# One layer of a hybrid diffusion trunk on one core: tile order of the output projection, gate on its products, stream slots, spread gathers, norm of x on GpSimd

## The chip, the core and the metric

The kernel runs on one core of a Trainium2 chip. The core has TensorE (PE, matmuls), VectorE (DVE), ScalarE (ACT), GpSimd (POOL) and SyncE (SP, which here only issues transfers), and 16 DMA engines that fill on-chip memory (SBUF) from HBM. Matmul results land in PSUM. The metric is device time in microseconds (us) of one execution; the median of several runs is compared.

## The reference, cut to what matters

One layer (DEPTH = 1) on 512 latent tokens of width 1024, with 256 context tokens, in float32.

```python
h  = modulate(rms_norm(x, norm1_g), sh1, sc1)          # shifts, scales, gates from c @ w_mod
p  = h @ w_in                                          # q, k, v, hyena, fourier, three gates
m  = sigmoid(ga)*ya + sigmoid(gh)*yh + sigmoid(gf)*yf  # three branches @ w_branch
x  = x + g1 * (m @ w_out)                              # the output projection
h2 = modulate(rms_norm(x, norm2_g), sh2, sc2)
aff = softmax(h2 @ w_router)                           # 512 x 16
top_w, top_i = top_k(aff.T, 64)                        # each of 16 experts chooses 64 tokens
y  = (silu(h2[top_i] @ w_gate) * (h2[top_i] @ w_up)) @ w_down * top_w
x  = x + g2 * scatter_add(y)
return rms_norm(x, final_g)
```

w_gate, w_up and w_down hold 16 experts of three 1024 x 2048 matrices: 24 MB (of 2^20 bytes) per expert, 384 MB in all, each read once.

## The kernel before, in words

**Stages.** First comes an opening (lines 327 to 526) whose order on SP, ACT, DVE and PE is that of the program (`tc.manual_schedule`; POOL is not in it): the filters of the long convolution, the products of c with the first third of w_mod (`mod1`, eight blocks of 1 MB), the sums of squares of x (`square`), the inverse root (`rsqrt`, Newton steps without a table) and the scaling of x (`xscale`, even tiles on DVE, odd ones on ACT). `mrow` copies the product row out of PSUM once `mod1(7)` is done; the shifts and scales A1, B1 and then `hT` follow from it. From line 609 on a planner (the tile framework) orders each engine's instructions by its own estimate. Then come projections, long convolutions, attention and the merge (`merge`, lines 1178 to 1204).

**Output projection.** The merged rows lie as T3a (row tiles 0 and 1) and T3b (row tiles 2 and 3), each in a high and a low part; so does w_out, in four column blocks of 256: `WO[0]` in the slot T1_0, `WO[1]` in T1_1, `WO[2]` in wsp, `WO[3]` in mpart. `wo_load(q)` (line 1160) loads 1 MB of w_out, multiplies it by the gate g1 on POOL (line 1167), and splits it into high (ACT, line 234) and low (DVE, line 235). `wout(c, t)` (line 1230) does one 128 x 256 product in 24 matmuls (8 k's of three), adds it to x on DVE (line 1238) and squares it on ACT. The program first runs column blocks 0 and 1 for all four row tiles, then 2 and 3 for all. In between lie the transposes `x1T`, router products `logits`, `norm2`, `affinity`, `affT`, and `best(t)` (eight rounds of top-8 and replace on DVE; row tile 1 needs the result of row tile 0, and 2 that of 1). After the last `best` come threshold, slot numbers and the first one-hot gather.

**The weight stream.** 386 blocks, nearly all of 1 MB, numbered in the order of use: 8 of w_gate, 8 of w_up, 8 of w_down per expert (0 to 7, 8 to 15, 16 to 23 for expert 0). `loads()` (line 1098) says which slot each goes to, `prefetch` issues them on SP in that order. A load waits on SP until the slot's former content has been read, and all later loads wait behind it. Two-block slots (T2b, T2a, T1_0, T1_1, wsp, T3a, T3b) and the ring (three single blocks) come round; acc, mpart and xtra serve once. The slots hold 22 blocks at first. After that a cycle has 16 blocks, with two ring loads in it. A pair that starts at an even block is one 2 MB transfer, else it is two of 1 MB (lines 1126 to 1131). The memory of mpart becomes the pool `moe` (line 1406), in which the hidden rows of expert 0 lie.

**Experts.** `up(e)` multiplies the gathered rows with 16 blocks (line 1401), `down(e)` with 8 (line 1437). `gather(pr)` picks the rows of two experts by 64 one-hot matmuls, in eight steps (line 1372); `gather(0)` runs inside `up(0)`, every other one is run as a whole between the two experts of a pair (line 1466). After each pair the results are scattered (line 1481) and added.

Of the kernel before, what the change touches and what calls it, by code (L numbers as in the profile page):

```python
# [19 lines left out]
D = 1024  # L20
# [172 lines left out]
def _body(tc, nc, es, a, out, dbg, stop):  # L193
# [94 lines left out]
    def rsqrt(pool_, out_, ms, shape, pre, E=None, tag=""):  # L288

        E = E or V  # L290

        t, y, z = (pool_.tile(shape, F32, name="rq" + tag + n) for n in "tyz")
        E.tensor_scalar(t, ms, pre, EPS, op0=OP.mult, op1=OP.add)
        E.tensor_scalar(y.bitcast(I32), t.bitcast(I32), -0.5, float(0x5F3759DF), op0=OP.mult, op1=OP.add)

        def yyt():
            if shape[1] == 1:
                E.tensor_scalar(z, y, y, t, op0=OP.mult, op1=OP.mult)
            else:
                E.tensor_mul(z, y, y)  # L300
                E.tensor_mul(z, z, t)

        for c in (3.0, 12.0):
            yyt()
            if shape[1] == 1:
                E.tensor_scalar(y, z, c, y, op0=OP.subtract, op1=OP.mult)
            else:
                E.scalar_tensor_tensor(y, z, c, y, op0=OP.subtract, op1=OP.mult)
        yyt()
        E.tensor_scalar(z, z, -1.0 / 8192.0, 3.0 / 32.0, op0=OP.mult, op1=OP.add)  # L310
        E.tensor_mul(out_, z, y)
# [193 lines left out]
    rsqrt(ep, XR[0], MS[0], [128, 4], 1.0 / D, tag="4")  # L505
    mod1(4)
    next(sp)
    for t in range(4):
        xscale(t)
# [3 lines left out]
    drain(sp)  # L513
    mod1(7)
# [583 lines left out]
    def loads():  # L1098


        first = [("T2b", 0), ("T2a", 2), (None, 4), (None, 5), (None, 20), ("acc", 6), ("T1_0", 8), ("T1_1", 10),
                 ("T3a", 16), ("mpart", 12), ("wsp", 14), ("T3b", 18), ("xtra", 21)]
        yield from first
        j = 22
        while j < len(stream):
            for tag in ("T2b", "T2a", None, None, "T1_0", "T1_1", "wsp", "T3a", "T3b"):
                yield tag, j
                j += 1 if tag is None else 2
# [51 lines left out]
    def wo_load(q):  # L1160

# [5 lines left out]
        G.tensor_mul(w_, w_, g1b[:, None, cs_].to_broadcast([128, 8, 256]))  # L1167
# [62 lines left out]
    def wout(c, t):  # L1230
# [3 lines left out]
        for k in range(8):  # L1234
            mm3(o[:, :256], *(x_[:, k, t % 2 * 128:(t % 2 + 1) * 128] for x_ in MT[t // 2]), W[0][:, k], W[1][:, k], k == 0, k == 7)
            if k == 3:
                yield
        V.tensor_add(x1[:, t, cs_], x1[:, t, cs_], o[:, :256])
# [48 lines left out]
    for t in range(4):  # L1287
        drain(wout(0, t))
        if t:
            x1T(t - 1, 0)  # L1290
        drain(wout(1, t))
        if t:
            logits(t - 1, 0)
    prefetch(2)
    for t in range(4):
        w_ = wout(2, t)
        next(w_)
        x1T(t - 1 if t else 3, 1 if t else 0)
        drain(w_)
        if t:  # L1300
            logits(t - 1, 1)
            affinity(t - 1)
        else:
            logits(3, 0)
        drain(wout(3, t))
        if t == 1:
            prefetch(1)
        norm2(t)
        if t == 3:
            x1T(3, 1)  # L1310
        if t:
            affT(t - 1)
            best(t - 1)
    logits(3, 1)
    affinity(3)
    affT(3)
    prefetch(3)
# [70 lines left out]
    def up(e):  # L1388
        gat = gather(0) if e == 0 else iter(())
        es_ = slice((e % 2) * CAP, (e % 2 + 1) * CAP)  # L1390
        acc_ = []
        for nm in ("pa", "pu"):
            o = pbig(nm) if e < NE - 1 or nm == "pa" else [pmm(nm), pmm(nm)]
            for k in range(8):
                next(gat, None)
# [61 lines left out]
    for pr in range(8):  # L1457
# [7 lines left out]
        if pr < 7:  # L1465
            drain(gather(pr + 1))
        else:
            fgb = K1n[:, :1024]
            nc.scalar.dma_start(fgb[0:1], a["rows"][:, 1024:2048])
            spread(fgb, -0.5)  # L1470
# [99 lines left out]
```

## Time and profile before

| what | us |
|---|---|
| median of 3 runs (1482.6 to 1487.5) | 1484.34 |
| the profiled execution | 1482.58 |
| its span, first to last instruction | 1480.8 |
| PE busy | 1344.8 |
| DVE busy | 501.1 |
| ACT busy | 287.6 |
| POOL busy | 131.7 |

The profile is of one execution. Busy time is a sum over stages with different limits, so the argument goes by stage: by windows of the span, by the timeline of one engine, and by the chain of work that ended last. DMA share is the mean busy share of the 16 DMA engines; GB/s counts 10^9 bytes, so 1 MB of the stream is 1.049 of its megabytes. "Idle before <- X" names what an engine waited for.

### The profile page before, as it was taken

To read this page: it belongs to the slowest core of one execution; us is meant where nothing else is said; L and a number is where in the kernel's file an instruction comes from. 1 tells how busy PE (TensorE), PEld (TensorE's weight loads), DVE (VectorE), ACT (ScalarE), POOL (GpSimd) and SP (SyncE) were. 2 spreads that over 40 slices of the span, in tenths; PEclk is the share of its full clock that TensorE was granted. 3 is DMA by queue.
4 is the path that set the end of the run, shared out by engine and by line. 5 is a ranking of instruction groups with operands and counts; after the bars stand their busy time and mean duration, and the time that the engine had idled before them with its cause. 6 is when DMAs were issued, how large, how long until landed. Compare 5 with 4: busy or idle time off the path is not lost.

```text
span 1480.8 us, 16061 instructions
## 1 busy us (share of the span) xinstructions
PE 1344.8 (91%) x6659; PEld 713.8 (48%) x6659; DVE 501.1 (34%) x980; ACT 287.6 (19%) x513; POOL 131.7 (9%) x131
## 2 busy tenths in 40 slices
PE   5899999999998979999999889988979988989896
PEld 2666678777787953433434323323423423423233
DVE  5867677666557361121121021111101201201123
ACT  5554235444333210100000000000000000000003
POOL 2043431000114010000000000000000000000002
PEclk9999999999999989999999999999999999999998
DMA  9425795110525658899999999999999999999994
GB/s 380 179 76 154 295 307 116 58 56 30 208 90 187 249 223 337 333 430 428 429 430 432 429 430 430 430 430 431 430 431 429 430 430 430 430 430 430 429 430 193
DMA packets 50658, 478.66 MB, mean 323 GB/s; under 512 B 5517, under 2 KB 10255, under 8 KB 16666
## 3 DMA queue, kind: packets, MB, share of 16 engines
q1 hardware_dynamic: 46008, 464.20, 76.0%
q0 software_dynamic: 2752, 9.05, 2.4%
q10 hardware_dynamic: 1826, 4.40, 0.8%
q8 instruction: 52, 0.85, 0.2%
q14 instruction: 20, 0.16, 0.0%
HBM read 473.02 MB, written 4.21 MB: 322 GB/s over the span
## 4 chain that ended last, share of the span: by engine, by line
PE 50%; DMA 41%; DVE 5%; ACT 2%; issue 1%; POOL 0%; ACTq 0%; DVEq 0%; SPq 0%
DMA rawT<-in_wu_dram 11%; DMA rawT<-in_wd_dram 9%; DMA rawwsp<-in_wu_dram 7%; PE py L1437 6%; PE pmm L229 6%; PE pmm L230 6%; PE pmm L231 6%; PE pu L1401 6%; PE pa L1401 5%; DMA rawT3a<-in_wu_dram 4%; DMA rawT2a<-in_wg_dram 2%; DMA rawwsp<-in_wg_dram 2%; DMA rawT2b<-in_wu_dram 2%; PE gx L1372 2%; DMA ld<-in_wmod_dram 2%; PE pmm L1056 2%
## 5 line engine op out<-in xcount | busy, mean ns | idle before, releaser
L1415 DVE TENSOR_TENSOR hid<-hid,pu 128x512 f32<-128x512 f32 x32 | 20.6, 684 | 453.9 <-PE pu L1401 441.4
L229 PE MATMUL pmm<-T,wsp 128*128 128x512 f32 x288 | 115.6, 404 | 1.3 <-DVE ht L594 1.3
L231 PE MATMUL pmm<-T,wsp 128*128 128x512 f32 x288 | 113.3, 393 | 2.2 <-DVE wsp L235 2.2
L230 PE MATMUL pmm<-T,wsp 128*128 128x512 f32 x288 | 113.4, 394 | 1.3 <-DVE T L235 1.3
L1414 ACT ACTIVATE hid<-pa 128x512 f32<-128x512 f32 x32 | 17.4, 594 | 421.0 <-PE pa L1401 406.5
L1372 PEld LDWEIGHTS gx<-vt,x 128*128 128x128 f32 x512 | 62.2, 195 | 29.3 <-issue 18.7
L1357 POOL TENSOR_SCALAR vt<-iota,slot,rs 128x64 f32<-128x64 f32 x16 | 10.3, 669 | 735.6 <-PE stp L1452 717.0
L1372 PE MATMUL gx<-vt,x 128*128 128x128 f32 x512 | 69.8, 289 | 5.2 <-DVE vt L1357 1.9
L1443 DVE TENSOR_TENSOR Y<-py,g2b 64x512 f32<-64x512 f32 x30 | 20.7, 689 | 154.1 <-PE py L1437 139.6
L235 DVE TENSOR_TENSOR wsp<-ld,wsp 128x1024 fp32r<-128x1024 f32 (+1 forms) x39 | 54.4, 1403 | 42.3 <-ACT wsp L234 42.1
L1437 PE MATMUL py<-rawT,hidT 128*64 128x512 f32 x224 | 52.3, 612 | 14.8 <-DMA rawT<-in_wd_dram 14.8
L229 PEld LDWEIGHTS pmm<-T,wsp 128*128 128x128 f32 x288 | 53.9, 188 | 21.6 <-issue 9.5
L1481 PE MATMUL sc<-Y,st 128*128 128x512 f32 (+1 forms) x128 | 57.0, 598 | 5.6 <-DVE Y L1443 5.6
L231 PEld LDWEIGHTS pmm<-T,wsp 128*128 128x128 f32 x288 | 54.2, 188 | 16.1 <-DVE wsp L235 2.6
L230 PEld LDWEIGHTS pmm<-T,wsp 128*128 128x128 f32 x288 | 54.4, 189 | 13.6 <-DVE T L235 1.9
L1423 ACT ACTIVATE hidT<-hp 128x512 f32<-128x512 f32 x16 | 9.6, 597 | 264.4 <-PE hp L1418 145.5
L234 ACT ACTIVATE wsp<-ld 128x1024 fp32r<-128x1024 f32 (+1 forms) x39 | 41.8, 1078 | 51.8 <-PE pmm L230 30.6
L1481 PEld LDWEIGHTS sc<-Y,st 128*128 128x128 f32 (+1 forms) x128 | 23.5, 189 | 39.5 <-issue 26.4
L1485 DVE TENSOR_TENSOR acc<-acc,sc 128x512 f32<-128x512 f32 x56 | 38.2, 687 | 10.9 <-PE sc L1481 10.9
L1437 PEld LDWEIGHTS py<-rawT,hidT 128*64 128x64 f32 x224 | 16.6, 140 | 50.2 <-issue 39.3
L1401 PE MATMUL pu<-rawT,xg 128*64 128x512 f32 x128 | 32.7, 654 | 6.2 <-DMA rawT<-in_wu_dram 6.2
L1401 PE MATMUL pu<-rawT,K1n 128*64 128x512 f32 x128 | 30.7, 600 | 7.9 <-DMA rawT<-in_wu_dram 7.9
(563 smaller groups left out, 2372.9 us busy)
## 6 DMA issues: line engine op xcount, KB each, us to landing
rawT<-in_wu_dram SPq DMA_DIRECT2D x16, 2048.0 KB, 33.9
rawT<-in_wg_dram SPq DMA_DIRECT2D x16, 2048.0 KB, 34.0
rawT<-in_wd_dram SPq DMA_DIRECT2D x14, 2048.0 KB, 29.2
ld<-in_wmod_dram SPq DMA_DIRECT2D x24, 1024.0 KB, 6.7
ld<-in_win_dram SPq DMA_DIRECT2D x19, 1024.0 KB, 5.7
ld<-in_wg_dram SPq DMA_DIRECT2D x18, 1024.0 KB, 34.0
rawT2a<-in_wg_dram SPq DMA_DIRECT2D x9, 2048.0 KB, 33.5
rawwsp<-in_wu_dram SPq DMA_DIRECT2D x9, 2048.0 KB, 28.7
```

Of the source, the lines that this page charges most:

```text
L229: mm(o, ah, bh, start=first, stop=False)
L230: mm(o, ah, bl, start=False, stop=False)
L231: mm(o, al, bh, start=False, stop=last)
L234: keep(A.activation(hi, src, AF.Copy))
L235: keep((eng or V).tensor_sub(lo, src, hi.bitcast(F32)))
L1056: mm(o[64 * g:64 * g + 64], vt[:, k, kv * 64:kv * 64 + 64], PT[h - 1 + g][:, k, :], start=k == 0, stop=k == 5)
L1372: mm(o[:, k % 4], x1[:, t, k * 128:(k + 1) * 128], oh[:, t], start=t == 0, stop=t == 3)
L1401: mm(ob[64 * hf:64 * hf + 64], xg[:, k, es_], w_[:, (2 * b + hf) * 512:(2 * b + hf + 1) * 512], start=k == 0, stop=k == 7)
L1437: mm(o[64 * dh:64 * dh + 64, :], hcol(hT_, fb), w_[:, i * 1024 + dh * 512:i * 1024 + (dh + 1) * 512], start=fb == 0, stop=fb == 15)
L1443: V.tensor_mul(Y2[es2, dh * 512:(dh + 1) * 512], o[64 * dh:64 * dh + 64], M["g2b"][64 * dh:64 * dh + 64, dh * 512:(dh + 1) * 512])
L1481: mm(o, st[ks, t * 128:(t + 1) * 128], Y2[ks, ds_], start=True, stop=True)
L1485: V.tensor_add(acc[:, t, ds_], acc[:, t, ds_], o)
```

## The change

1. In the opening, `rsqrt` for x runs on POOL instead of DVE, where the fused subtract-and-multiply becomes two instructions; the four `xscale` move behind `mod1(6)` and the last filter planes.
2. `wo_load` no longer multiplies by g1. `wout` multiplies its product by g1 on DVE into a scratch tile and adds that to x: two DVE instructions instead of one.
3. The projection runs row tiles 0 and 1 through all four column blocks first. The first two products do k = 0 to 6 before either does k = 7. `x1T`, `logits`, `norm2`, `affinity`, `affT` and `best` follow each row tile as it is complete. Loads are issued as T3a, T1_0, T1_1, wsp, mpart and T3b come free, in this order.
4. The stream's slots: T3a takes blocks 6 and 7, then T1_0, T1_1, wsp, mpart, T3b take 8 to 17; acc, which serves once, takes 18 and 19. The cycle has a third ring load: 17 blocks.
5. `gather(pr + 1)` runs inside `up` of the pair's second expert, one step at every second k.

```diff
@@ rsqrt
+            elif E is G:
+                E.tensor_scalar(z, z, c, None, op0=OP.subtract)
+                E.tensor_mul(y, z, y)
@@ the opening
-    rsqrt(ep, XR[0], MS[0], [128, 4], 1.0 / D, tag="4")
+    rsqrt(ep, XR[0], MS[0], [128, 4], 1.0 / D, G, tag="4")
     mod1(4)
     next(sp)
-    for t in range(4):
-        xscale(t)
     mod1(5)
     next(sp)
     mod1(6)
     drain(sp)
+    for t in range(4):
+        xscale(t)
     mod1(7)
@@ loads
-        first = [("T2b", 0), ("T2a", 2), (None, 4), (None, 5), (None, 20), ("acc", 6), ("T1_0", 8), ("T1_1", 10),
-                 ("T3a", 16), ("mpart", 12), ("wsp", 14), ("T3b", 18), ("xtra", 21)]
+        first = [("T2b", 0), ("T2a", 2), (None, 4), (None, 5), (None, 20), ("acc", 18), ("T3a", 6), ("T1_0", 8),
+                 ("T1_1", 10), ("wsp", 12), ("mpart", 14), ("T3b", 16), ("xtra", 21)]
...
-            for tag in ("T2b", "T2a", None, None, "T1_0", "T1_1", "wsp", "T3a", "T3b"):
+            for tag in ("T2b", "T2a", None, None, "T3a", "T1_0", "T1_1", "wsp", "T3b", None):
@@ wo_load
-        G.tensor_mul(w_, w_, g1b[:, None, cs_].to_broadcast([128, 8, 256]))
@@ wout
-    def wout(c, t):
+    def wout(c, t, stop=4):
...
         for k in range(8):
+            if k == stop:
+                yield
             mm3(o[:, :256], *(x_[:, k, t % 2 * 128:(t % 2 + 1) * 128] for x_ in MT[t // 2]), W[0][:, k], W[1][:, k], k == 0, k == 7)
-            if k == 3:
-                yield
-        V.tensor_add(x1[:, t, cs_], x1[:, t, cs_], o[:, :256])
+        d_ = flat(vt)[:, (c + t) % 2 * 256:((c + t) % 2 + 1) * 256]
+        V.tensor_mul(d_, o[:, :256], g1b[:, cs_])
+        V.tensor_add(x1[:, t, cs_], x1[:, t, cs_], d_)
@@ the order (the old loops are removed)
+    w0, w1 = wout(0, 0, 7), wout(0, 1, 7)
+    for w_ in (w0, w1, w0, w1):
+        next(w_)
+    inside, behind, later = [], [], []
+    for c, t in ((1, 0), (1, 1), (2, 0), (3, 0), (2, 1), (3, 1), (0, 2), (1, 2), (2, 2), (3, 2), (0, 3), (1, 3), (2, 3), (3, 3)):
+        w_ = wout(c, t)
+        next(w_)
+        for f_, *as_ in inside:
+            f_(*as_)
+        drain(w_)
+        for f_, *as_ in behind:
+            f_(*as_)
+        inside, behind, later = [], later, []
+        if c % 2:
+            inside = [(x1T, t, c // 2)]
+            behind.append((logits, t, c // 2))
+        if c == 3:
+            norm2(t)
+            behind.append((affinity, t))
+            later = [(affT, t), (best, t)]
+        if (c, t) in ((3, 1), (0, 3), (1, 3), (2, 3)):
+            prefetch(1)
+    for f_, *as_ in inside + behind:
+        f_(*as_)
+    affT(3)
     prefetch(2)
@@ up
-        gat = gather(0) if e == 0 else iter(())
+        gat = gather(0) if e == 0 else gather(e // 2 + 1) if e % 2 and e < NE - 1 else iter(())
...
-                next(gat, None)
+                if e == 0 or k % 2:
+                    next(gat, None)
@@ between the experts of a pair
-        if pr < 7:
-            drain(gather(pr + 1))
-        else:
+        if pr == 7:
```

## Rows read from the trace of the kernel before

**Rows 1.** The page's second part: DMA busy tenths and GB/s in 40 equal slices of the span (37 us each).

```profile
DMA  9425795110525658899999999999999999999994
GB/s 380 179 76 154 295 307 116 58 56 30 208 90 187 249 223 337 333 430 428 429 430 432 429 430 430 430 430 431 430 431 429 430 430 430 430 430 430 429 430 193
```

**Rows 2.** Windows of the span: stretch, its length, busy us (and instructions) of PE, PEld, DVE, ACT, POOL, then the granted TensorE clock, DMA share, GB/s. First the start of the experts, then the stretch up to the end of the stream, then the end.

```profile
555.00:620.00 65.00, 64.17 (x332) 28.19 (x332) 10.94 (x34) 6.22 (x12) 1.28 (x2) 1.00 0.85 322
620.00:640.00 20.00, 19.15 (x90) 6.42 (x86) 1.14 (x2) 1.09 (x2) 0.00 (x0) 1.00 1.01 430
640.00:1440.00 800.00, 724.87 (x3334) 271.49 (x3334) 123.82 (x253) 40.52 (x76) 7.67 (x12) 0.99 1.01 430
...
1455.00:1460.00 5.00, 5.00 (x30) 2.87 (x30) 1.28 (x2) 3.37 (x10) 2.37 (x3) 1.00 0.31 127
```

**Rows 3.** The opening: the timeline of DVE (first and last instruction of `rsqrt`), of ACT (the two `xscale`, then `mrow`), and of POOL (the second filter sum; then first and last of the nine instructions of `norm2(1)` on POOL, much later). Columns: start us, us, engine, line, operation, out<-in, count, idle before.

```profile
35.76 0.17 DVE L293 TENSOR_SCALAR rq4t<-ms 128x4 f32<-128x4 f32 x1 [1.29 <-ACT T2b L385]
...
39.01 0.16 DVE L311 TENSOR_TENSOR xr<-rq4z,rq4y 128x4 f32<-128x4 f32 x1
...
39.21 2.19 ACT L390 ACTIVATE xa<-xa,xr 128x1024 f32<-128x1024 f32 x2 [2.99 <-DVE xr L311]
41.91 0.60 ACT L516 ACTIVATE mrow<-mod 128x512 f32<-128x512 f32 x1 [0.51 <-PE mod L366]
...
36.29 1.28 POOL L445 TENSOR_TENSOR Gt<-keep 128x512 f32<-128x512 f32 x1 [0.67 <-ACT keep L440]
...
514.68 0.20 POOL L293 TENSOR_SCALAR rqt<-ms 128x1 f32<-128x1 f32 x1 [43.08 <-DVE ms L1261]
...
517.68 0.19 POOL L311 TENSOR_TENSOR rs<-rqz,rqy 128x1 f32<-128x1 f32 x1
```

**Rows 4.** Around the last merge: the low splits of w_out blocks 0 and 1 and one add of the merge on DVE, the gate multiplications of blocks 2 and 3 on POOL, and the matmul behind PE's pause, from the engines' timelines; then a window behind it (columns as in rows 2).

```profile
457.46 2.29 DVE L235 TENSOR_TENSOR T<-ld,T 128x2048 fp32r<-128x2048 f32 x1 [1.35 <-ACT T L234]
460.40 6.00 DVE L235 TENSOR_TENSOR T<-ld,T 128x2048 fp32r<-128x2048 f32 x1 [0.64 <-ACT T L234]
...
467.03 4.27 DVE L1180 TENSOR_TENSOR mpart<-mpart,sg 128x512 f32<-128x512 f32 x1
...
472.49 0.68 DVE L1180 TENSOR_TENSOR mpart<-mpart,sg 128x512 f32<-128x512 f32 x1
...
459.49 4.76 POOL L1167 TENSOR_TENSOR ld<-ld,K1n 128x2048 f32<-128x2048 f32 x1 [5.77 <-DMA ld<-in_wout_dram]
465.04 5.72 POOL L1167 TENSOR_TENSOR ld<-ld,K1n 128x2048 f32<-128x2048 f32 x1 [0.79 <-DMA ld<-in_wout_dram]
...
471.81 0.58 PE L229 MATMUL pmm<-T,T3a 128*128 128x256 f32 x1 [6.24 <-ACT T3a L234]
...
471.80:476.40 4.60, 4.59 (x21) 4.56 (x22) 3.19 (x8) 3.45 (x5) 0.00 (x0) 0.51 0.79 337
```

**Rows 5.** The rest of the projection and the routing: a window over the last twelve of the 16 products, and one from there to the end of the last `best` (columns as in rows 2); from DVE's timeline the first and last instruction of `best(0)`, the instruction behind the last `best`, and one add of a product to x.

```profile
484.58:527.80 43.22, 43.22 (x370) 43.19 (x370) 19.22 (x87) 10.59 (x36) 4.82 (x18) 1.00 0.57 219
527.80:541.24 13.44, 8.09 (x32) 3.91 (x32) 12.26 (x65) 2.72 (x6) 0.00 (x0) 0.62 0.97 399
...
513.95 0.28 DVE L1283 MAX8 K1n<-K1n 16x8 f32<-16x128 f32 x1
...
519.60 0.26 DVE L1285 MATCH_REPLACE8 K1n<-K1n 16x128 f32<-16x128 f32 x1
...
541.24 0.22 DVE L1331 TENSOR_TENSOR both<-top,top 16x65 f32<-16x65 f32 x1
...
475.15 0.42 DVE L1238 TENSOR_TENSOR x<-x,pmm 128x256 f32<-128x256 f32 x1 [0.73 <-PE pmm L231]
```

**Rows 6.** Issues of stream loads on SP after the first filling (same columns; the issue comes when the slot is free and all earlier loads have been issued). They are those of blocks 22, 24, then 28 and 30, 32, 34, then 40.

```profile
554.13 0.33 SPq L1127 DMA_DIRECT2D rawT2b<-in_wd_dram  x1
561.80 0.33 SPq L1127 DMA_DIRECT2D rawT2a<-in_wg_dram  x1
...
573.69 3.76 SPq L1127 DMA_DIRECT2D rawT<-in_wg_dram  x2
583.99 0.33 SPq L1127 DMA_DIRECT2D rawwsp<-in_wu_dram  x1
591.12 0.33 SPq L1127 DMA_DIRECT2D rawT3a<-in_wu_dram  x1
...
613.51 0.33 SPq L1127 DMA_DIRECT2D rawT2a<-in_wd_dram  x1
```

**Rows 7.** The same stretch on PE and ACT: blocks 16 and 17, blocks 20 and 21, and the start of `gather(1)` on PE; the first use of the hidden rows of expert 0 on ACT.

```profile
587.42 3.65 PE L1437 MATMUL py<-rawT3a,hidT 128*64 128x512 f32 x16
...
594.34 3.60 PE L1437 MATMUL py<-ld,hidT 128*64 128x512 f32 x16
...
603.21 3.14 PE L1372 MATMUL gx<-vt,x 128*128 128x128 f32 x24
...
581.24 1.09 ACT L1414 ACTIVATE hid<-pa 128x512 f32<-128x512 f32 x2 [14.47 <-PE pu L1401]
```

**Rows 8.** PE in the middle of the stream, where it waits for arrivals: starts on block pairs, each with its wait. The last two are six blocks apart, two of them single ring loads.

```profile
1072.25 3.65 PE L1401 MATMUL pu<-rawwsp,K1n 128*64 128x512 f32 x16 [0.67 <-DMA rawwsp<-in_wu_dram]
...
1086.87 3.65 PE L1401 MATMUL pu<-rawT2b,K1n 128*64 128x512 f32 x16 [1.21 <-DMA rawT2b<-in_wu_dram]
...
1101.58 3.65 PE L1437 MATMUL py<-rawT,hidT 128*64 128x512 f32 x16 [1.71 <-DMA rawT<-in_wd_dram]
```

More of the change, by code (lines that the diff above doesn't have):

```diff
@@ L1285, in best @@
                 V.match_replace(wk[i], m_, wk[i], -1.0)
[L1287 to L1293, printed above, removed]
-    prefetch(2)
[L1295 to L1302, printed above, removed]
-        else:
[L1304 to L1317, printed above, removed]
+    w0, w1 = wout(0, 0, 7), wout(0, 1, 7)
[23 more added lines that the diff above has]
+    affT(3)
+    prefetch(2)
     p_ = pmm("clock")
@@ L1464, in _body @@
             gp = es.enter_context(pool("gat", side="right"))
-        if pr < 7:
-            drain(gather(pr + 1))
-        else:
+        if pr == 7:
             fgb = K1n[:, :1024]
```

## The prediction

> **What bounds the kernel now.** I read the slices first. In the page's second part the DMA row stands at 9 and the GB/s row at 428 to 432 from slice 18 to slice 39; before that it is mostly below 340 [rows 1]. The windows sharpen this: from 555 to 620 the queue moves 322 GB/s, from 620 on 430, with a DMA share of 1.01 for 800 us, and the stream ends between 1455 and 1460 [rows 2]. The reader is to see two regimes. From 620 on the 16 DMA engines are the bound, whatever PE does, and nothing in the diff changes how many bytes are left. So the end moves only by what is done before 620: by work that starts the stream's regime earlier, and by DMA idle time that is closed before it. PE is busy 64.17 of 65 us in the window that still has idle DMA [rows 2], so there the stream waits for slots that PE has yet to read. Everything ahead of the experts is a chain of computation, so a microsecond there counts one for one.
>
> **The change part by part.** Durations are from the profiled execution of 1482.58 us (span 1480.8); the median of the runs is 1.76 us above it, and I add that at the end.
>
> *Opening.* `rsqrt` runs from 35.76 to 39.17 on DVE, then ACT scales two tiles (2.19 us), then comes `mrow` at 41.91, which the shifts and `hT` need [rows 3]. In the new order ACT still does both `xscale` ahead of `mrow`, so moving them back buys nothing unless the roots are early. The new chain is 14 POOL instructions. The nearest row is the nine-instruction chain of `norm2` on POOL, 514.68 to 517.87, 0.355 us each: 14 x 0.355 = 5.0 us [rows 3]. Roots at 35.74 + 0.1 + 5.0 = 40.8, `mrow` at 43.0: 1.1 us late. If POOL puts the filter sum of 1.28 us in front, 2.4 us late. Shortest case: 14 x 0.28 (about the step of the chain's cheap instructions) gives roots at 39.7 and no delay; a gain would need roots before 39.7. Longest: the sum in front and each instruction twice as long, some 6 us. I take **+1.6** (0 to +6). DVE gets 3.4 us free, but it has nothing to fill them with: its next steps hang on `mrow`.
>
> A rule speaks against this part: GPSIMD Engine Reference of the Trainium skill, Engine selection, puts elementwise work on VectorE and GpSimd at about half its speed for two inputs. By it 3.4 us would become 6.8, the delay some 2.9 us and the sum 1.3 us worse; the trace's POOL chain, 0.355 us each, speaks for the smaller figure.
>
> *Gate off the weights.* PE pauses 6.24 us before the matmul at 471.81 [rows 4]. The chain behind that pause: the low split of w_out block 1 takes 6.00 us where block 0's takes 2.29, and the merge's add takes 4.27 us where the next takes 0.68; both lie under POOL's gate multiplications (459.49 to 464.25 and 465.04 to 470.76) [rows 4]. Without these, DVE's chain is 460.40 + 2.29 = 462.7, then merge 6 (0.68 + 0.68, then ACT 0.42 and DVE 0.42) to 465.1 and merge 7 to 467.0. PE needs k = 6 of the first product at 463.3 + 18 x 0.12 = 465.4 and, with two products of 21 matmuls ahead, k = 7 only at 463.3 + 42 x 0.12 = 468.3. So the pause goes: **-6.2**. Behind it PE ran 21 matmuls in 4.60 us at a granted clock of 0.51, which is the 1.2 GHz level; at the rate of the later window (370 in 43.22 us) they take 2.5 [rows 4, 5]. Without the pause: **-2.1**. Bounds: -6 if PE still stops briefly for k = 7, -8.3.
>
> What the gate adds: 16 more DVE instructions of 0.42 us (the add's own row [rows 5]), 6.7 us in all. DVE is busy 19.22 of 43.22 us in the projection [rows 5], so they fit; a late row tile's `x1T` follows 1.44 us (12 matmuls) behind a product whose two instructions end after some 0.9 us.
>
> *Row-tile order.* PE's work in the projection is the same. What changes is the tail. Before, PE ends at 527.8 and the last `best` at 541.24: 13.4 us, of which DVE is busy 12.26 [rows 5]. Some 5 us of that is the rest of `best(2)`; `best(0)` takes 513.95 to 519.86 [rows 5], the wider ones some 6.7. Now `best(2)` starts two products before the end and is nearly done by then, so 7.3 us of DVE work stay in the tail. But they are a chain (add, square, root, softmax, transpose, `best(3)`) whose waits on ACT and PE the rest of `best(2)` used to cover: between 1.2 us (DVE's idle of before) and some 6; I take 4, so 11.3. And since DVE is nearly full from 491 on (18.9 of `best`, 6.7 of products, 3 of softmax in 28 us) I give 1.1 back: 12.4, **-1.0** (-4 to +1.5).
>
> *Pool of expert 0.* mpart now holds blocks 14 and 15, not 12 and 13, so the hidden rows' memory is free two blocks (3.4 us) later. ACT's first use of it at 581.24 [rows 7] becomes about 584.5 and the next product 1 us later; PE fills part of it with expert 1: **+0.8** (0 to +1).
>
> *Slots and spread gather.* The last slot of the first filling (xtra) is loaded when the slot numbers are there, before and after, so I keep the clock of before from there on and move PE's reads only where the change moves them. A block costs (1086.87 - 1072.25) / 6 = 2.44 us of DMA [rows 8] and 1.72 us of PE (3.43 per pair, from the starts at 587.42 and 594.34 [rows 7]). A transfer starts at the later of the DMA's end and issue + 0.8 us (an estimate; with it the walk reproduces before).
>
> Before: pairs issued at 554.13, 561.80, (two ring loads at 563.5), 573.69 (two pairs), 583.99, 591.12, ..., 613.51 [rows 6]. After 555 the DMA stands still 2.6 us (560.0 to 562.6), 2.1 (572.4 to 574.5), 0.6, 2.2, 0.4 and 7.3 (607.1 to 614.4): 15.2 us. By bytes the window gives 65 x (1 - 322/430) = 16.3 [rows 2], so the walk holds. The last hole is `gather(1)`: it starts at 603.21 [rows 7] and blocks 24 and 25 are read only at 613.4.
>
> After: block 28 waits for blocks 6 and 7 (read at 572.6) instead of 8 and 9, block 30 for 8 and 9 (573.6), 32 for 10 and 11, 34 for 12 and 13 (580.4) instead of 14 and 15, 36 for 16 and 17 (590.9), 38 for 20 (596.1), 39 for 22 and 23 (601.4). Blocks 24 and 25 are read at 603.2 + 1.7 + 1.2 + 1.7 = 607.8. The walk: 22 at 555 to 560; 24 to 27 at 562.6 to 572.4; 28 at 573.7; 30, 32, 34 without a hole to 593.3; 36 to 598.2; 38 to 600.6; 39 at 602.4 to 607.3; 41 at 608.9 to 613.8; then closed. Holes: 2.6 + 1.3 + 1.8 + 1.6 = 7.3. **-7.9** (-9 to -3, if PE's order differs). Later gathers hide: PE needs some 103 us per pair of experts, the DMA 117 (48 x 2.44). Later slots, too: block 64 would start at 665 and its slot is free at 664.5, the tightest place.
>
> T1_0 comes free only at about 508 instead of 494; ten blocks then load from 509 to 534, 7 us before the next slot (block 1) is read, so this costs nothing; beyond 7 us it would.
>
> *Split pairs.* A cycle of 17 makes every second cycle's seven pairs start at odd blocks: about 73 pairs become two 1 MB loads. From 1086.87 to 1101.58 six blocks, two of them single, take 14.71 us; the six from 1072.25, all in pairs, 14.62 [rows 8]. That is at most 0.09 us per split pair, 6.6 us in all; ring loads at 430 GB/s elsewhere show none. I take **0** (0 to +6.6).
>
> **Sum:** +1.6 - 6.2 - 2.1 - 1.0 + 0.8 - 7.9 = -14.8 us: 1467.8 for the profiled execution, 1469.5 against the median. Forecast 1469.
>
> **Rivals.**
> - *The head start comes, the holes stay* (1477): if PE reads expert 0 in another order, or a later slot wait replaces the closed ones, -7.9 falls away. Against it: PE's reads are fixed by block rates. Chance 0.16.
> - *DVE becomes the bound of the projection* (1474): `best` stands ahead of gated products in DVE's queue, PE's four PSUM buffers fill, and the tail is 4 us longer instead of 1 shorter. For it: 28.6 us of work in 28. Chance 0.09.
> - *Split pairs cost, so the kernel is slower* (1491): at 0.3 us each, 73 x 0.3 = 22 us in the bound regime. It decides from 14.8 / 73 = 0.20 us per pair on; the row shows 0.09 at most. Chance 0.06. The Trainium skill, DMA: Bandwidth & Descriptors, section Bandwidth, gives 341 GB/s for a 1 MB transfer and 425 for 16 MB, which points to this side; rows 8 show queued 1 MB loads at nearly the rate of pairs, so the trace disagrees.
> - *The change doesn't free the merge* (1485): the 6.00 and 4.27 us have another cause than POOL, the pause stays, and the holes stay too. Against it: both lie exactly under POOL's spans [rows 4]. Chance 0.07.
>
> **How the numbers follow.** The forecast's own case, 1463 to 1475, has 0.62. The range 1461 to 1480 adds the first two rivals. Some 0.3% (4.5 us) is what a measurement can tell from no change. Faster by more: 0.62 + 0.09 + most of 0.16 = 0.85; within: 0.09; slower: 0.06.
>
> **What the new profile would show.** No POOL work near 460, the split of block 1 near 2.3 us, no pause of PE and no window at 0.5 clock before the projection; `mrow` 1 to 2 us later; threshold some 8 us earlier; hardly any DMA share under 0.8 between xtra and the end; 430 GB/s after that. A rate under 428 there, or a threshold no earlier, would make the prediction wrong.

## The result, and the profile after

| | before | after |
|---|---|---|
| median us (7 runs each) | 1482.97 | 1473.61 |
| lowest to highest | 1481.45 to 1487.5 | 1471.19 to 1478.07 |
| ratio, 95% interval | | 0.9936 [0.992, 0.9953] |
| the profiled execution | 1482.58 | 1474.33 |
| its span | 1480.8 | 1472.5 |

The kernel became 9.4 us faster; forecast were 14.8 (1469, range 1461 to 1480, reckoned from the 1484.34 of the first three runs). The span is shorter by 8.3 us, and two issues on SP divide it. The first load of the stream (`rawT2b`) goes out 3.28 us later than before (399.41 for 396.13). The load into xtra, which waits for the slot numbers, goes out 5.38 us earlier (538.48 for 543.86). From there to the end of the span it takes 934.0 us instead of 936.9. So 3.28 were lost in and behind the opening, 8.66 won between the two issues, and only 2.9 behind the second, where 7.1 were expected (the slots' 7.9 less the 0.8 of the pool).

**Opening.** Timelines of the kernel after, POOL's roots and then `mrow` on ACT (columns as in rows 3):

```profile
35.77 0.19 POOL L293 TENSOR_SCALAR rq4t<-ms 128x4 f32<-128x4 f32 x1 [0.20 <-ACT T2b L388]
...
36.89 0.24 POOL L308 TENSOR_SCALAR rq4z<-rq4z 128x4 f32<-128x4 f32 x1
37.09 1.29 POOL L448 TENSOR_TENSOR Gt<-keep 128x512 f32<-128x512 f32 x1
38.34 0.20 POOL L309 TENSOR_TENSOR rq4y<-rq4z,rq4y 128x4 f32<-128x4 f32 x1
...
40.63 0.20 POOL L314 TENSOR_TENSOR xr<-rq4z,rq4y 128x4 f32<-128x4 f32 x1
40.86 2.19 ACT L393 ACTIVATE xa<-xa,xr 128x1024 f32<-128x1024 f32 x2 [4.71 <-POOL xr L314]
42.95 0.57 ACT L519 ACTIVATE mrow<-mod 128x512 f32<-128x512 f32 x1
```

The reader is to see the step from one root instruction to the next, 0.28 us, and the filter sum of 1.29 us in the middle of the chain. The roots end at 40.83 and `mrow` starts 1.04 us later than in rows 3.

**Around the last merge.** DVE's two low splits, then the adds of the merge, from its timeline (compare rows 4):

```profile
460.48 2.29 DVE L235 TENSOR_TENSOR T<-ld,T 128x2048 fp32r<-128x2048 f32 x1 [1.53 <-ACT T L234]
463.68 2.29 DVE L235 TENSOR_TENSOR T<-ld,T 128x2048 fp32r<-128x2048 f32 x1 [0.91 <-ACT T L234]
466.60 0.69 DVE L1181 TENSOR_TENSOR mpart<-mpart,sg 128x512 f32<-128x512 f32 x1
...
468.48 0.68 DVE L1181 TENSOR_TENSOR mpart<-mpart,sg 128x512 f32<-128x512 f32 x1
```

Windows over the same place and over the projection (columns as in rows 2):

```profile
465.00:475.00 10.00, 10.00 (x79) 9.71 (x78) 8.13 (x11) 5.15 (x7) 0.00 (x0) 1.00 1.02 391
481.60:525.00 43.40, 43.20 (x368) 42.84 (x366) 28.50 (x123) 10.19 (x34) 5.17 (x18) 1.00 0.48 186
```

The 6.00 and 4.27 us of rows 4 are 2.29 and 0.69. PE neither pauses nor runs at the lower level: 10.00 of 10 us busy at a granted clock of 1.00, which is the 2.4 GHz level, where rows 4 had 6.24 us of idle time and then 0.51. The times of rows 4 also show how DVE was held up. Its split, begun at 460.40 under POOL's multiplication, ended 2.15 us behind that multiplication's end (466.40 and 464.25); its add, begun at 467.03 under the next one, ended 0.54 us behind it (471.30 and 470.76). Alone they take 2.29 and 0.68. So DVE all but stood still until POOL was done. DVE is busier in the projection (28.50 us for 19.22 in rows 5, with two row tiles' `best` now inside it), and PE is still full. The last `best` is followed by `both` at 535.93 instead of 541.24.

**The stream.** The DMA and GB/s rows of the page's second part, 37 us a slice (compare rows 1):

```profile
DMA  9424786111445489999999999999999999999994
GB/s 379 182 77 154 286 279 151 64 47 41 145 155 203 147 345 382 391 396 419 430 428 428 431 425 432 424 430 427 431 427 426 431 425 431 425 429 429 429 428 194
```

Windows of the kernel after at 10 to 40, 40 to 80, 80 to 110, 110 to 140, 140 to 200 and 300 to 900 us behind the issue for xtra:

```profile
548.48:578.48 30.00, 28.60 (x141) 11.06 (x139) 2.98 (x12) 1.46 (x4) 0.00 (x0) 1.00 0.91 359
578.48:618.48 40.00, 39.55 (x190) 15.96 (x191) 5.45 (x13) 4.79 (x9) 1.28 (x2) 1.00 0.99 394
618.48:648.48 30.00, 29.06 (x146) 11.56 (x147) 4.58 (x13) 1.51 (x3) 0.00 (x0) 1.00 0.99 410
648.48:678.48 30.00, 30.00 (x122) 10.46 (x120) 6.91 (x10) 1.08 (x2) 0.00 (x0) 1.00 0.97 399
678.48:738.48 60.00, 58.80 (x298) 24.41 (x296) 8.11 (x23) 4.11 (x8) 1.28 (x2) 1.00 1.01 426
838.48:1438.48 600.00, 540.13 (x2434) 195.76 (x2432) 93.29 (x185) 29.53 (x55) 5.12 (x8) 0.99 1.01 428
```

The last column is to be read downwards. A hole is time in which the DMA engines lack work, seen as a rate below 430 GB/s. The deep hole of before (316 GB/s in the second stretch counted from its own issue for xtra) has become 394. But the third and fourth stretch, full before (433 and 428), now read 410 and 399, and the rest runs at 428, not 430. The holes were closed and others came.

### The profile page after: what moved, and what is told of

It reads as the page before. It is cut to its first block, busy times and chain, and to the rows that moved or that the text cites. A ratio compares the mean times of both kernels' runs of the same rounds, so it can differ in the third digit from the quotient of the medians.

```text
span 1472.5 us, 16253 instructions
## 1 busy us (share of the span) xinstructions
PE 1354.8 (92%) x6659; PEld 712.1 (48%) x6659; DVE 495.1 (34%) x984; ACT 287.7 (20%) x513; POOL 114.8 (8%) x141
## 4 chain that ended last, share of the span: by engine, by line
PE 48%; DMA 42%; DVE 5%; ACT 3%; issue 1%; POOL 1%; ACTq 0%; SPq 0%; DVEq 0%
DMA rawwsp<-in_wu_dram 6%; PE pmm L229 6%; PE pmm L230 6%; PE pmm L231 6%; PE pa L1402 6%; PE pu L1402 5%; PE py L1438 5%; DMA ld<-in_wd_dram 4%; DMA rawT2b<-in_wu_dram 4%; DMA rawT<-in_wd_dram 3%; DMA rawT3a<-in_wd_dram 3%; DMA ld<-in_wg_dram 3%; DMA rawT<-in_wu_dram 3%; PE gx L1371 2%; DMA rawT2b<-in_wg_dram 2%; DMA ld<-in_wu_dram 2%
## 5 line engine op out<-in xcount | busy, mean ns | idle before, releaser
L1416 DVE TENSOR_TENSOR hid<-hid,pu 128x512 f32<-128x512 f32 x32 | 20.7, 684 | 419.8 <-PE pu L1402 406.2
L1444 DVE TENSOR_TENSOR Y<-py,g2b 64x512 f32<-64x512 f32 x30 | 20.7, 689 | 161.8 <-PE py L1438 147.3
L1402 PE MATMUL pu<-rawT,K1n 128*64 128x512 f32 x152 | 36.6, 599 | 3.3 <-DMA rawT<-in_wu_dram 3.2
L1438 PE MATMUL py<-ld,hidT 128*64 128x512 f32 x168 | 38.9, 596 | 0.5 <-DMA ld<-in_wd_dram 0.5
L1028 DVE TENSOR_REDUCE sm<-pbig 128x1 f32<-128x768 f32 x32 | 30.5, 955 | 17.2 <-PE pbig L1026 17.1
```

The costliest lines, as they stand in the source:

```text
L1028: V.tensor_reduce(sm[:, 0:1], pb[:, :768], axis=AX.X, op=OP.max)
L1402: mm(ob[64 * hf:64 * hf + 64], xg[:, k, es_], w_[:, (2 * b + hf) * 512:(2 * b + hf + 1) * 512], start=k == 0, stop=k == 7)
L1416: V.tensor_mul(hid[:, bs], hid[:, bs], acc_[1][b] if e == NE - 1 else acc_[1][:, bs])
L1438: mm(o[64 * dh:64 * dh + 64, :], hcol(hT_, fb), w_[:, i * 1024 + dh * 512:i * 1024 + (dh + 1) * 512], start=fb == 0, stop=fb == 15)
```

## Experiments

Each kernel ran in five rounds beside the kernel before, whose median was 1482.5 to 1482.8. The tables use three numbers from each profile: the time from the first stream load to the issue for xtra ("routing"), from there to the end of the span ("stream"), and the DMA time lost there against 430 GB/s, which is the sum over ten windows of length x (1 - GB/s / 430). Each profile is of one execution, and the executions of one kernel lie up to 9 us apart, so a small step is believed only where medians and profile agree.

**1. No pair split.** Odd cycles begin with a ring load, so that every pair starts at an even block.

```diff
-  for tag in ("T2b", "T2a", None, None, "T3a", "T1_0", "T1_1", "wsp", "T3b", None):
+  for tag in (("T2b", "T2a", None, None, "T3a", "T1_0", "T1_1", "wsp", "T3b", None) if j % 2 == 0 else
+              (None, "T2b", "T2a", "T3a", "T1_0", "T1_1", "wsp", "T3b", None, None)):
```

Expected: 

> The changed kernel, with every second cycle of slots starting on a ring load, so that all pairs of blocks start even and no pair is split into two 1 MB loads; still 17 blocks and three ring loads a cycle. Theory (split pairs cost DMA rate: 428 GB/s from 700 to 1440 against 430 before): the rate in that stretch returns to 430, the time falls by 740 x 2/430 = 3.4 us, to about 1470 (1468 to 1472). Rival (the lower rate comes from something else, such as more loads in flight): rate stays at 428, time within 1 us of the changed kernel's 1473.6. The hole at 660 us behind the first scatter stays in both.

Measured: 1489.42 us, 1.0042 [1.0027, 1.0057]. Windows of this kernel:

```profile
545.00:620.00 75.00, 73.15 (x346) 29.52 (x346) 8.76 (x25) 6.84 (x13) 1.20 (x2) 0.98 0.78 309
620.00:700.00 80.00, 78.21 (x362) 30.10 (x362) 14.81 (x32) 4.15 (x8) 1.28 (x2) 1.00 0.85 357
700.00:1400.00 700.00, 622.21 (x2881) 234.48 (x2879) 101.93 (x218) 34.99 (x67) 6.39 (x10) 1.00 1.01 430
```

Late in the stream the rate is back at 430 (428 in the kernel after), so whole pairs do run faster. The time is a miss for theory and rival alike, and the design was at fault: the moved ring load, block 39, reuses the slot of block 26, only 13 blocks back, and every load behind it in SP's queue waits too. SP's timeline, blocks 38 and 39, then 40:

```profile
592.39 13.92 SPq L1135 DMA_DIRECT2D ld<-in_wu_dram  x2
606.36 0.42 SPq L1131 DMA_DIRECT2D rawT2b<-in_wd_dram  x1
```

Block 40 goes out at 606.36 instead of 595.39, and the first two windows read 309 and 357 where the kernel after has 364 and 409.

**2 and 3. The old opening**, with the change otherwise whole, and with kernel 1.

```diff
-    rsqrt(ep, XR[0], MS[0], [128, 4], 1.0 / D, G, tag="4")
+    rsqrt(ep, XR[0], MS[0], [128, 4], 1.0 / D, tag="4")
     mod1(4)
     next(sp)
+    for t in range(4):
+        xscale(t)
...
     drain(sp)
-    for t in range(4):
-        xscale(t)
```

Expected of 2: 

> The changed kernel with the opening of before (root on DVE, scalings ahead of the sixth product). Theory (the opening costs 3.3 us: 1.0 until mrow, the rest because PE's pause of 3.75 us there is followed by matmuls at half clock): the first stream load is issued near 396.1 instead of 399.4 us and the time falls by 3.3 us to about 1470.3. Rival (the delay is absorbed later, where the stream is bound by DMA): first stream load near 396, but the end within 1 us of the changed kernel.

Expected of 3: 

> Both of the other two edits together: opening of before, and no split pairs. If the two costs are separate and both are real, they add: 3.3 + 3.4 = 6.7 us less than the changed kernel, about 1467. If only one of them is real, 1470; if neither, 1473.6.

Measured: 2 gives 1472.03 us, 0.9925 [0.9907, 0.9944], against 1473.61 for the whole change; 3 gives 1488.33, 1.0033 [1.002, 1.0046], against 1489.42. Both are 1.1 to 1.6 us better than with the new opening, within the intervals. 3 misses all three of its values, since it carries the late block 39 of kernel 1. 2 comes out between its two: the 3.28 us by which the first stream load had come late did not come back (398.25 instead of the 396.1 expected). The opening needed more executions; they are put together below.

**4. The gate alone.** The kernel before with nothing but the gate moved to the products.

```diff
-        G.tensor_mul(w_, w_, g1b[:, None, cs_].to_broadcast([128, 8, 256]))
...
-        V.tensor_add(x1[:, t, cs_], x1[:, t, cs_], o[:, :256])
+        d_ = flat(vt)[:, (c + t) % 2 * 256:((c + t) % 2 + 1) * 256]
+        V.tensor_mul(d_, o[:, :256], g1b[:, cs_])
+        V.tensor_add(x1[:, t, cs_], x1[:, t, cs_], d_)
```

Expected: 

> The kernel before, with the gate moved from w_out to the products, and nothing else: order of the projection, slots, gathers and opening as before. Theory (GpSimd's gate multiplications stretch DVE's split and add and so make PE's pause of 6.24 us): the split of w_out block 1 takes 2.3 us, PE's pause shrinks to under 2 us, no half clock behind it, slot numbers some 7 us earlier, time about 1476 (1474 to 1478). Rival (the pause has another cause): pause and time as before, 1483.

Measured: 1473.09 us, 0.9931 [0.9916, 0.9946]. SP's timeline gives the first stream load and the load into xtra:

```profile
393.55 0.33 SPq L1127 DMA_DIRECT2D rawT2b<-in_wg_dram  x1
...
533.60 0.33 SPq L1131 DMA_DIRECT2D ld<-in_wd_dram  x1
```

DVE's splits of w_out blocks 0 and 1, and windows over the last merge and the first products, show the cause at work by itself:

```profile
454.61 2.29 DVE L235 TENSOR_TENSOR T<-ld,T 128x2048 fp32r<-128x2048 f32 x1 [1.53 <-ACT T L234]
457.81 2.29 DVE L235 TENSOR_TENSOR T<-ld,T 128x2048 fp32r<-128x2048 f32 x1 [0.91 <-ACT T L234]
...
455.00:465.00 10.00, 10.00 (x62) 8.91 (x61) 8.41 (x11) 4.80 (x7) 0.00 (x0) 1.00 0.78 267
465.00:475.00 10.00, 10.00 (x87) 10.00 (x86) 7.59 (x11) 5.17 (x12) 0.00 (x0) 1.00 0.98 389
```

No split is stretched, POOL does nothing, PE has no pause and no half clock. Routing takes 140.05 us, 7.68 less than before. The time is 0.9 us below the range expected. This one edit brings what the whole change brings; the other four together bring nothing.

**5. Gathers whole again**, with the change otherwise whole.

```diff
-        gat = gather(0) if e == 0 else gather(e // 2 + 1) if e % 2 and e < NE - 1 else iter(())
+        gat = gather(0) if e == 0 else iter(())
...
+        if pr < 7:
+            drain(gather(pr + 1))
```

Expected: 

> The changed kernel with every gather run as a whole between the two experts of a pair, as before. Theory (spreading closes the DMA hole of about 6 us at the first of these gathers, but most of that is given back when the DMA runs into the 17-block lead behind the first scatter): DMA stands still around 605 us in place of the hole at 660 us, and the time is within 3 us of the changed kernel, 1473 to 1477. Rival (the spreading carries the stream's gain): 1479 or more.

Measured: 1479.43 us, 0.9973 [0.9959, 0.9986]: 5.8 us slower than the whole change. From 40 to 80 us the rate falls to 323 GB/s (394 in the kernel after), while from 80 to 200 us only 0.5 us are lost instead of 4.1: the later hole goes, as the theory said, but the time goes to the rival. Its nine executions lie in two groups, four near 1475 and five from 1479.4 to 1482.3; the profile is of the first group, so no trace shows what parts them, and 5.8 is not to be taken as the worth of spreading. So spreading is worth something, and something else in the change costs as much.

**6 and 7. The slots.** In 6 the cycle has two ring loads again (16 blocks, no pair split), with the change's order of the first filling. In 7 that order is taken back, too: acc serves early (blocks 6 and 7).

```diff
-  first = [..., ("acc", 18), ("T3a", 6), ("T1_0", 8), ("T1_1", 10), ("wsp", 12), ("mpart", 14), ("T3b", 16), ("xtra", 21)]
+  first = [..., ("acc", 6), ("T3a", 16), ("T1_0", 8), ("T1_1", 10), ("wsp", 14), ("mpart", 12), ("T3b", 18), ("xtra", 21)]
-  for tag in ("T2b", "T2a", None, None, "T3a", "T1_0", "T1_1", "wsp", "T3b", None):
+  for tag in ("T2b", "T2a", None, None, "T1_0", "T1_1", "wsp", "T3a", "T3b"):
```

Expected of 6: 

> The changed kernel with two ring loads a cycle instead of three: 16 blocks, all pairs even, so none is split, at the price of one block of lead. Theory (split pairs cost 428 against 430 GB/s over 750 us, 3.4 us; one block of lead is worth at most 2.4 us and only at the first scatter): rate 430 again, time 1471 to 1473. Rival (the lead matters more than the rate): rate 430, but more holes before 700 us, time 1475 or more.

Expected of 7: 

> The changed kernel with the slot order of before (blocks 6 and 7 in acc, 16 and 17 in T3a, 18 and 19 in T3b, a cycle of 16, no split pairs), the order of the projection, the gate, the spread gathers and the opening as changed. Theory (the slot order closes holes before 620 us that come back behind the scatter, and the split pairs cost 3.4 us): rate 430, more holes before 620, time within 3 us of the changed kernel. Rival (late blocks in one-time slots are a net gain): 1477 or more.

Measured: 6 gives 1475.12 us, 0.9939 [0.9923, 0.9956]; 7 gives 1469.14, 0.9917 [0.99, 0.9934]. Both stream at 430 GB/s to the end. 6 gains nothing, as its rival said: its shorter cycle comes with more holes (339 GB/s from 40 to 80 us). 7 is 4.5 us faster than the whole change, more than the 3 its theory allowed, and far from its rival: the new slots are a loss. The two intervals overlap a little; kernels 9 and 2 below are a second pair, with 3.5 us.

**8. All pairs split.** Kernel 4, in which from block 22 on every pair is two loads.

```diff
-            if len(js) == 2 and stream[j][1] == 0:
+            if len(js) == 2 and stream[j][1] == 0 and j < 22:
```

Expected: 

> The kernel before with the gate on the products (1473.1), and from block 22 on every pair is loaded as two 1 MB transfers, with slots and order unchanged. Theory (each split pair costs some 0.045 us of DMA, 3.4 us for 73): all 160 pairs split cost about twice that, the rate from 700 to 1400 falls to 426 and the time rises by 7 us, to 1480. Rival (the 428 GB/s of the changed kernel have another cause): rate 430, time 1473.

Measured: 1477.43 us, 0.9963 [0.9948, 0.9977]. A late window of it:

```profile
837.00:1437.00 600.00, 541.70 (x2408) 188.30 (x2406) 91.16 (x182) 28.92 (x54) 5.11 (x8) 1.00 1.01 427
```

The rate is 427 at a full DMA share (430 in kernel 4), and the kernel takes 4.3 us longer for some 160 split pairs: 0.03 us each, about 2 us for the 73 of the change. That split pairs cost is confirmed, at some two thirds of the size expected.

**9 to 11. The parts that pay, one by one**, on the slots and the opening of before, with the gate on the products: 9 has row-tile order and spread gathers (kernel 7 with the opening of kernel 2), 10 the order alone (9 with the gathers of kernel 5), 11 the spread gathers alone (kernel 4 with the inverse of the diff of 5).

Expected of 9: 

> The changed kernel with the slots, their order and the cycle of 16 blocks of before, and with the opening of before (roots on DVE, the xscale ahead of mod1(5)): what is left of the change is the gate on the products, the row-tile order and the spread gathers. Theory (slots give nothing, the opening costs some 0.5 to 1 us): 1468.4, and 430 GB/s over the second half of the stream. Rival (the opening is hidden): 1469.1, as with the old slots alone.

Expected of 10: 

> The kernel above without the spread gathers: gate and row-tile order alone, gathers whole between the experts of a pair. Theory (the order is worth the 1.0 us by which it brings the threshold forward): 1472, 139.0 us from the first stream load to the issue for xtra, and a hole near gather(1) as before. Rival (the stream turns it into nothing): 1473.1, as with the gate alone.

Expected of 11: 

> Gate on the products and the spread gathers alone, in the column-block order, slots and opening of before. Theory (spreading closes the hole of gather(1), the gain is not given back where the cycle keeps 16 blocks and pairs whole): 1473.1 less 3.5 to 5, so 1468 to 1469.6, with over 400 GB/s from 40 to 80 us behind the issue for xtra. Rival (what is closed comes back as holes behind the first scatter): 1473, with under 420 GB/s somewhere from 80 to 200 us.

**12. The third ring load alone**, added to kernel 9: 17 blocks, split pairs, old order of the first filling.

```diff
-  for tag in ("T2b", "T2a", None, None, "T1_0", "T1_1", "wsp", "T3a", "T3b"):
+  for tag in ("T2b", "T2a", None, None, "T1_0", "T1_1", "wsp", "T3a", "T3b", None):
```

Expected: 

> The kernel with the gate on the products, the row-tile order, the spread gathers and the slots of before, its cycle given the third ring load at its end: 17 blocks, so every second cycle's pairs are split, but acc still takes blocks 6 and 7. It parts the two halves of the slots' edit. Theory (the split pairs' rate is the smaller half, some 2 us of the 3.5 to 4.5 that the slots cost): 1470.5, with 427 to 428 GB/s from 300 us behind the issue for xtra. Rival (the cycle is the whole cost): 1472 to 1473. Second rival (only the order of the first filling costs, the longer lead pays for the rate): 1468.5.

| kernel | median us | ratio [95%] | routing | stream | lost at 0 to 80, 80 to 200, 200 to 900 us |
|---|---|---|---|---|---|
| before | 1482.97 | 1 | 147.73 | 936.9 | 25.1, -0.1, 0.5 |
| 4: gate | 1473.09 | 0.9931 [0.9916, 0.9946] | 140.05 | 934.6 | 23.6, -0.1, 0.0 |
| 11: gate, spread | 1470.16 | 0.9914 [0.9898, 0.9931] | 140.09 | 935.4 | 19.7, 1.3, 0.0 |
| 10: gate, order | 1472.64 | 0.9942 [0.9923, 0.9961] | 139.06 | 935.3 | 21.9, -0.1, 0.0 |
| 9: gate, order, spread | 1468.48 | 0.9903 [0.9888, 0.9918] | 139.07 | 930.5 | 16.6, 0.7, 0.0 |
| 12: 9 and third ring load | 1470.28 | 0.9921 [0.9906, 0.9936] | 139.03 | 932.2 | 14.4, 1.7, 3.0 |
| 2: 9 and all of the slots | 1472.03 | 0.9925 [0.9907, 0.9944] | 139.06 | 934.9 | 15.9, 3.6, 3.0 |
| the whole change | 1473.61 | 0.9936 [0.992, 0.9953] | 139.07 | 934.0 | 13.9, 4.1, 3.0 |

Kernel 9 is the best of all: 14.2 us faster than before, with an interval that ends below that of the whole change. Read down the table, the gate gives 9.4 us (against 1482.51 in its own rounds), the order 0.5 to 1.7, spreading 2.9 to 4.2. The third ring load takes 1.8 back, the new order of the first filling another 1.8, the opening 0.7 to 1.6 (kernel 9 against 7, 2 against the whole change). The small steps lie within the intervals of single kernels. The stream column holds some 1.5 us of a lower clock in its first 10 us for the kernel before and for kernels 2, 6 and 11 (last section). With that taken off kernel 2, the column gives 1.7 us for the third ring load (932.2 against 930.5) and 1.2 for the new order of the first filling. Kernels 9 and 12 came out as their theories said (1468.4 and 1470.5), 10 between its two (1472, 1473.1), and 11 a little above its range, at 1470.16 instead of 1469.6 at most. Its rate from 40 to 80 us is 376 GB/s, not over 400, and the sign of its rival, under 420 somewhere from 80 to 200 us, is there in a small way (416, 1.3 us lost); its time is far from the rival's 1473. Windows of kernel 10, then of kernel 9, at 40 to 80, 80 to 110, 110 to 140 and 300 to 900 us:

```profile
574.71:614.71 40.00, 40.00 (x209) 18.13 (x210) 6.74 (x21) 4.53 (x9) 1.28 (x2) 1.00 0.82 317
614.71:644.71 30.00, 29.00 (x136) 9.84 (x132) 2.33 (x4) 1.37 (x3) 0.00 (x0) 1.00 1.01 431
644.71:674.71 30.00, 30.00 (x124) 10.61 (x124) 6.55 (x10) 1.08 (x2) 0.00 (x0) 1.00 1.01 428
...
834.71:1434.71 600.00, 529.94 (x2427) 196.08 (x2425) 92.69 (x185) 29.52 (x55) 5.12 (x8) 1.00 1.01 430
```

```profile
575.08:615.08 40.00, 40.00 (x195) 16.01 (x196) 4.22 (x11) 4.85 (x9) 1.28 (x2) 1.00 0.95 372
615.08:645.08 30.00, 29.06 (x146) 11.39 (x144) 4.58 (x13) 1.05 (x2) 0.00 (x0) 1.00 1.00 429
645.08:675.08 30.00, 30.00 (x122) 10.46 (x120) 6.91 (x10) 1.08 (x2) 0.00 (x0) 1.00 1.01 421
...
835.08:1435.08 600.00, 532.49 (x2456) 198.51 (x2454) 93.59 (x186) 29.53 (x55) 5.11 (x8) 0.99 1.01 430
```

Spreading alone lifts 317 to 372, and most of what it closes stays closed (429, 421, then 430: 5.3 us fewer up to 80 us, 0.8 of them given back by 200).

## Why the prediction was right or wrong

**What bounds the kernel** was read rightly: in every kernel the stream's regime sets the end.

**Gate, -8.3.** Right. By the routing time of kernel 4 -7.7, by its median -9.4, with the three signs named (split 2.29, no pause, no stretch at 0.51).

**Row-tile order, -1.0.** Right for the routing, which goes from 140.05 to 139.06. Less than that may arrive at the end: by the medians of 4 and 10 it is 0.5, and the stream column grows by 0.7. In the first 10 us behind the issue for xtra kernel 10 moves 200 GB/s and kernel 4 moves 125, so in the new order earlier loads are still under way there. The prediction put that at nothing. The rival in which DVE becomes the bound did not come, with PE busy 43.20 of 43.40 us.

**Opening, +1.6.** Right in sign and near in size, by other parts: the 14 instructions step by 0.28 us, not 0.355, and the filter sum did come in between. By a rule weighed there (GPSIMD Engine Reference of the Trainium skill, Engine selection: about half of VectorE's speed for two inputs) the chain would take, as an estimate, twice DVE's 3.4 us. Without the sum it took 5.06 - 1.29 = 3.8 us here, so for tiles this small the trace disagrees. What the opening costs has to be read between executions with the same clock. Of the 14 profiles eight kept a full clock from 39 to 54 us, but five of these lost it from 92 to 102 us (0.83; last section). Among those five, the three with the old opening issue the first stream load at 395.65 to 396.40 (mean 396.1), the two with the new one at 396.79 and 397.31: 1.0 us later, as `mrow` is. The three with a full clock in both stretches, all with the old opening, issue it at 393.55 to 394.75. The kernel after lost its clock in both stretches, the kernel before only in the second, so the rest of the 3.28, some 2.3, goes with the clock from 39 to 54 us.

**Pool, +0.8.** ACT's first use of the hidden rows moved from 581.24 to 577.79, that is from 37.38 to 39.31 us behind the issue for xtra: 1.93 later, which is the 3.4 worked out less the 1.5 that `gather(0)` gained (below). PE's next wait shows it (start, length, idle before), first in the kernel before, then after:

```profile
584.80 0.66 PE L1418 MATMUL hp<-packb,hid 128*128 128x128 f32 x4 [0.83 <-DVE hid L1415]
...
578.93 1.07 PE L1402 MATMUL pa<-rawT2a,K1n 128*64 128x512 f32 x2 [1.85 <-ACT hid L1415]
```

That is 1.0 us more, near the 0.8 put down. What of it reaches the end was not measured by itself.

**Slots and spread gather, -7.9, and split pairs, 0: these two terms were mis-sized.** Up to 80 us behind xtra the holes shrink from 21.9 us (kernel 10, which has the same order of the projection) to 13.9: 8.0, as worked out. But the term was booked whole, and 4.1 + 3.0 us of it are given back later, in two places. Between kernel 10 and the kernel after, which have the same clock in `gather(0)` too, the stream column falls by 1.3 us and no more (935.3 to 934.0).

The first is around the first scatter. The prediction walked the stream up to block 41, took it as closed from there, and named block 64, at 665 us, as "the tightest place". That place has the largest of the new holes. PE reads no weights during a scatter (651.72 to 658.85), so no slot comes free. SP's timeline of the kernel after, two neighbouring lines, the second with the load of block 64:

```profile
649.25 0.33 SPq L1130 DMA_DIRECT2D rawT3a<-in_wu_dram  x1
660.74 3.76 SPq L1130 DMA_DIRECT2D rawT<-in_wd_dram  x2
```

and the scatter on PE:

```profile
651.72 7.13 PE L1480 MATMUL sc<-Y,st 128*128 128x512 f32 x16
```

Between these two issues lie 11.49 us; then the queue is empty, as the window shows (DMA share 0.75, 221 GB/s):

```profile
660.00:664.00 4.00, 4.00 (x22) 1.31 (x20) 0.00 (x0) 0.00 (x0) 0.00 (x0) 1.00 0.75 221
```

This window alone loses 1.9 of the 4.1 us. The rest lies in smaller holes from 618 to 738 us, with 344 GB/s from 640 to 644 us.

Up to 200 us the whole change loses 18.0 us, kernel 9 with the old slots 17.3: the slots move the holes and close none. Kernel 5, the slots without spreading, says so too: 21.1 against 21.8 in kernel 10. What closes them for good is spreading (22 to 17). Kernel 6 says the same from the other side: with the new order and a cycle of 16 blocks, spread as well, it loses 20.7 + 1.7, which is 5.1 more than kernel 9. Some 1.5 of that is the lower clock of its first 10 us, so the new first filling costs some 3.6 us of holes; kernel 2, at the same lower clock, loses 19.5, so the third ring load buys 2.9 back for its 3.0 of rate. By the medians the first filling costs 6.0 in one pair (6 against 7) and 1.8 in another (2 against 12), so its size is not settled. Why the late blocks in acc and mpart make the later cycles tighter was not taken apart further.

The second is the split pairs, given 0 (0 to 6.6). They cost 0.02 to 0.04 us each: 1.7 by the stream column (kernel 12 against 9, with what the longer lead gives already in it), 3.0 by bytes. The rows had shown 0.09 at most, and zero was chosen because single ring loads elsewhere showed none. A rule weighed there, DMA: Bandwidth & Descriptors of the Trainium skill, section Bandwidth, gives 341 GB/s for transfers of 1 MB and 425 for 16 MB, measured there on transfers issued from GpSimd. The direction is the one measured, the size is not: 427 GB/s queued one behind the other (kernel 8), against 430 in pairs. The rival built on it (1491) did not come.

**The sum** by the profiled execution: opening +1.0, its clock +2.3, routing -8.7, stream -2.9, in all -8.3 where -14.8 were forecast. Of the 6.5 between them 4.2 are the stream (-7.1 forecast), 1.7 the opening with its clock, 0.6 the routing. Of the stream's 2.9 some 1.5 are the clock of `gather(0)` (last section), not the slots or the gathers. So the time lies in the forecast's own case, 1463 to 1475, but near its upper end, and more by the width of that case than by its terms. The rival in which the head start comes and the holes stay is half right: the holes of rows 6 closed, and others came later. The rival nearest in time (1474, DVE the bound) did not happen.

**The named signs** served. A rate under 428 late in the stream was to look bad, and it is 428, just at the edge. The sign that hardly any DMA share would lie under 0.8 did not come true: it is 0.75 behind the scatter.

## What to carry to other kernels

A stream that runs ahead of its reader has a fixed lead, the number of its slots. Closing an early hole only counts if the lead also lasts through the next stretch in which the reader frees nothing, so walk the queue past that stretch (here the first scatter) before booking the gain. A joined change should be priced part by part and run so: here one edit gave the whole gain, two more were worth 4.6 us on top, and the other two took 5.1 back.

## What was not expected of the hardware

**The clock behind a pause comes and goes.** Windows over 39 to 46 and 46 to 54 us of the kernel after (columns as in rows 2):

```profile
39.00:46.00 7.00, 3.25 (x20) 2.42 (x12) 2.91 (x7) 4.57 (x5) 1.33 (x7) 0.78 1.02 377
46.00:54.00 8.00, 7.15 (x23) 5.30 (x23) 7.89 (x14) 4.71 (x8) 0.00 (x0) 0.56 0.70 266
```

PE had waited 3.75 us for `mrow`; then the granted clock lies near the 1.2 GHz level. Kernel 1 has the same opening and a pause of 3.33 us, and shows 1.00 in both windows. Before shows 1.00, too, but kernel 2, with the same old opening, 0.62 and 0.69. Of 14 profiles six have the drop. With either opening it goes with the longer pauses. With the new one PE waited 3.73 to 4.27 us ahead of `mrow`'s product (in two parts in kernels 6 and 7) where the clock fell, 3.28 and 3.33 where it didn't. With the old one it waited ahead of the last filter plane, 2.02, 2.39 and 2.51 us where the clock fell, 1.26 to 2.13 where it didn't. As 2.02 and 2.13 stand the wrong way round, length alone doesn't decide.

Another place shows that better. Behind a pause of 2.16 or 2.17 us between 91 and 98 us, which all 14 profiles have, the clock fell in six and stayed in eight. Windows over 92 to 102 us of the kernel before, then of kernel 4:

```profile
92.00:102.00 10.00, 7.83 (x25) 4.57 (x25) 7.02 (x7) 5.86 (x8) 5.17 (x4) 0.83 0.53 116
92.00:102.00 10.00, 8.32 (x40) 5.75 (x41) 7.39 (x10) 7.06 (x11) 4.95 (x3) 1.00 0.57 130
```

With the old opening and a full clock from 39 to 54 us, the profiles with this second drop issue the first stream load 1.9 us later (395.65 to 396.40 against 393.55 to 394.75). What decides a drop was not settled.

**So does the clock of `gather(0)`.** From 545 to 550 us PE was granted 0.70 before and 1.00 after, and the T2b load comes 8.77 us behind the issue for xtra instead of 10.27. Kernels 4, 9, 10 and 12 show 8.77 to 8.78, kernels 2 and 6 10.38 and 10.41. Kernel 11, with the same order of the projection as 4, has 10.40 and, from 536 to 541 us:

```profile
536.00:541.00 5.00, 5.00 (x23) 2.59 (x22) 0.00 (x0) 0.46 (x1) 0.00 (x0) 0.66 0.46 184
```

So some 1.5 us of the stream column come from this alone: in the step from the kernel before to the kernel after, and in kernels 2, 6 and 11 against the others. No term of the prediction held it.
